# Two halves of the tokens, taken differently: five matmuls per weight tile in place of six in a float32 decoder step

## The chip, the cores and the metric

One core of a Trainium2 chip runs the whole program. Its engines are TensorE (PE in the profile; its weight loads have a row of their own, PEld), VectorE (DVE), ScalarE (ACT), GpSimd (POOL) and SyncE (SP, which issues most DMAs). Each engine works through its own queue in the order of issue, and semaphores tie the queues together. The metric is the time of one execution on the device, in microseconds; lower is better.

## The reference

One step of a two-layer decoder trunk over 520 tokens: a prompt of 512 and eight samples of one token each. Everything is float32. Cut to what matters:

```python
def layer(x, ...):
    x = x + 0.5 * swiglu_ffn(rms_norm(x, p['ffn1_norm']), wg, wu, wd)     # 1024 -> 2816 -> 1024
    h = rms_norm(x, p['mix_norm'])
    z = h @ p['w_in']              # 1024 -> 2560, split into
    # retention q, k, v, gate | windowed attention q, k, v | a gated pair for a convolution
    ...
    y = jnp.concatenate([o_r, o_a, o_c], axis=-1) @ p['w_out']           # 1024 -> 1024
    x = x + y
    x = x + 0.5 * swiglu_ffn(rms_norm(x, p['ffn2_norm']), wg2, wu2, wd2)
```

The outputs are the 520 tokens' vectors and the new states of retention, attention window and convolution.

## The kernel before

**Layout.** Activations lie with features on the 128 partitions and tokens along the columns: `x` is `[128, 8, 520]`. Weights come in tiles of 128 x 128, eight to a chunk of 512 KB, in the order of their use; a chunk is one DMA.

**Three terms for a product.** The big products are done on float32r operands, rounded forms of float32. To keep float32's accuracy each operand is split into two float32r parts, high and low: for weights by a ScalarE copy (line 185, `wh`) and a VectorE subtraction (line 192, `wl`), for the inputs likewise (`xh`, `xl`; lines 252 and 254, 222 and 223 for the FFN's hidden values `hs`). The product is `wh*xl + wh*xh + wl*xh`. `mm3` (line 206) issues this for one weight tile. An output tile `o` takes two banks of PSUM of 512 float32 columns each, and the 520 tokens are halved: 260 columns go to the first bank, 260 to the second (`HN` = 260). So a weight tile costs three terms times two halves, six matmuls, each with its own weight load:

```python
def mm3(o, w, vh, vl, first, last):
    for i, (a, b) in enumerate(((w[0], vl), (w[0], vh), (w[1], vh))):
        for s in range(2):
            nc.tensor.matmul(o[:, s, :HN], lhsT=a, rhs=b[:, s * HN : (s + 1) * HN], ...)
```

**Stages.** Each layer is an FFN, the mix and a second FFN. In an FFN (`ffn`, line 277) two groups of 11 blocks `f` are made: eight tiles of the gate into `og`, eight of the up projection into `ou`, then `silu(og * R) * (ou * R)` with the norm's factors `R` (lines 288 to 294), split into two parts. Then for each of eight output blocks `m` eleven tiles are summed and added to `x` (line 299). After the second group the next stage's input is prepared block by block (`prep`, line 250), and the next stage starts while the last blocks are being prepared.

The mix has 20 blocks of the input projection (`in_tile`, eight tiles each; RQ, RK, RV, RG of retention, AQ, AK, AV of attention, CA and CG of the convolution), the three mechanisms themselves, and the output projection in two halves of four tiles for each of eight blocks (`out`; steps `a` and `b`). Blocks that are scaled by `R` go through one VectorE operation that reads both banks (lines 380, 388, 484, 765, 851); others are copied by one ScalarE operation (lines 514, 663, 682); the convolution's pointwise product is split straight from PSUM (lines 461 and 464); the output projection is added to `x` at line 881. The order of all these steps on all queues is written out by hand in `ORDER` (line 80), where `t` is a part of the convolution's 62 taps on VectorE, `h` and `l` are the two halves of splitting the next chunk of weights, `s` and `n` are steps of the prompt's attention and of retention's norms.

**Buffers.** PSUM holds four output tiles `o` of two banks, which is all of it. Three chunks of raw weights and three of split ones are held. 20 units of 1040 columns hold intermediates.

Of the kernel before, what the change touches and what calls it, by code (L numbers as in the profile page):

```python
# [19 lines left out]
HN = NT // 2  # L20
FFN = 2816
# [9 lines left out]
# Columns of the packed per-layer parameters.  # L31
# [8 lines left out]
# Columns of the packed constants that depend on shapes alone.  # L40
# [37 lines left out]
# The mix's steps in the order of their issue. A step comes in parts, and each mention of it issues  # L78
# its next part. h and l stand for the two halves of the split of the next chunk of weights.
# [35 lines left out]
def step_kernel(ctx: ExitStack, tc: tile.TileContext, io: dict):  # L115
# [15 lines left out]
    xh = const.tile([128, KD, NT], F32R, name="xh")  # L131
    xl = const.tile([128, KD, NT], F32R, name="xl")
# [33 lines left out]
    # ---- the stream of 128x128 weight tiles in the order of their use: chunks are loaded, then  # L166
    # split exactly into two float32r parts ----
# [9 lines left out]
    def split_hi(i):  # L177
        """The first part of chunk i; the second is left pending."""
        if i == nxt[0] and i < NCH:
            nxt[0] += 1  # L180
            ensure_load(i)
            t, raw[i] = raw[i], None
            h = wspl.tile([128, CT * 128], F32R, tag="wh", name="wh")
            lo = wspl.tile([128, CT * 128], F32R, tag="wl", name="wl")
            nc.scalar.copy(h, t)  # L185
            spl[i] = (h, lo)
            pending.append((i, t))
# [18 lines left out]
    def mm3(o, w, vh, vl, first, last):  # L206
        for i, (a, b) in enumerate(((w[0], vl), (w[0], vh), (w[1], vh))):
            for s in range(2):
                nc.tensor.matmul(  # L209
                    o[:, s, :HN], lhsT=a, rhs=b[:, s * HN : (s + 1) * HN],  # L210
                    start=first and i == 0, stop=last and i == 2,
                )
# [37 lines left out]
    def prep(l, gain, k):  # L250
        g = prm(l, gain, k)
        nc.scalar.activation(xh[:, k], x[:, k], AF.Copy, scale=g)  # L252
        yield
        nc.vector.scalar_tensor_tensor(  # L254
            xl[:, k], x[:, k], g, xh[:, k].bitcast(F32), op0=ALU.mult, op1=ALU.subtract
        )
# [20 lines left out]
    def ffn(norm, after):  # L277
        for g in range(NG):
            hs = []
            for f in range(GF):  # L280
                first = g == 0 and f == 0
                og, ou = ptile(), ptile()
                for o, k in ffn_tiles(first, og, ou):
                    mm3(o, next_tile(), xh[:, k], xl[:, k], k == 0, k == KD - 1)
# [10 lines left out]
            for m in range(KD):  # L295
                o = ptile()
                for f in range(GF):
                    mm3(o, next_tile(), hs[f][:, 0], hs[f][:, 1], f == 0, f == GF - 1)
# [6 lines left out]
    def mix(l, after):  # L305
# [19 lines left out]
        def in_tile():  # L325
            o = ptile()
            for k in range(KD):
                mm3(o, next_tile(False), xh[:, k], xl[:, k], k == 0, k == KD - 1)
# [6 lines left out]
        # Each step is a generator, whose parts each keep to one engine for the most.  # L335
# [8 lines left out]
        def decayed():  # L344
            """The norm's factors times the decay of retention's queries."""
# [8 lines left out]
        def token_scales():  # L354
            """The norm's factors, and those with the decay of keys, with tokens on the partitions."""
# [13 lines left out]
        def conv_a(c):  # L369
# [10 lines left out]
            nc.vector.scalar_tensor_tensor(v2(a), o[:, :, :HN], 0.5, v2(R), op0=ALU.mult, op1=ALU.mult)  # L380
# [3 lines left out]
        def conv_g(c):  # L384
# [3 lines left out]
            nc.vector.tensor_mul(v2(g), o[:, :, :HN], v2(R))  # L388
# [32 lines left out]
        def conv_rest():  # L421
# [18 lines left out]
            hi, lo = two(unit(F32R)), two(unit(F32R))  # L440
            table(SILU)
            for c in range(2):
# [3 lines left out]
                nc.scalar.copy(hi[:, c], y[:, c])  # L446
            yield
            for c in range(2):
                nc.vector.tensor_sub(lo[:, c], y[:, c], hi[:, c].bitcast(F32))
            yield  # L450
            os = []
            for m in range(2):
                o = ptile()
                os.append(o)
                for k in range(2):
                    s = slice(k * 256 + m * 128, k * 256 + m * 128 + 128)
                    mm3(o, (pw[0][:, s], pw[1][:, s]), hi[:, k], lo[:, k], k == 0, k == 1)
            yield
            hl = two(unit(F32R)), two(unit(F32R))
# [19 lines left out]
        def att_qk(g):  # L479
            """Queries of a group or, where g is None, keys, with an RMS norm over each half of the partitions."""  # L480
# [3 lines left out]
            nc.vector.tensor_mul(v2(a), o[:, :, :HN], v2(R))  # L484
# [25 lines left out]
        def att_v():  # L510
# [3 lines left out]
            nc.scalar.copy(v2(av), o[:, :, :HN])  # L514
# [18 lines left out]
        def att_out():  # L533
            return get(att, "o", lambda: (two(unit(F32R)), two(unit(F32R))))
# [7 lines left out]
        def att_prompt(n):  # L542
            """128 queries: scores, softmax with the sink, values."""
# [54 lines left out]
            h_, l_ = (t[:, :, n * 128 : (n + 1) * 128] for t in att_out())  # L598
            src = o[:, 0, :256].rearrange("p (g t) -> p g t", g=2)
            nc.scalar.copy(h_, src)  # L600
            yield
            nc.vector.tensor_sub(l_, src, h_.bitcast(F32))
# [10 lines left out]
        def att_sample():  # L613
# [34 lines left out]
            for v in range(2):  # L648
                s = slice(64 * v, 64 * v + 64)
                src = o[s, 0, :32].rearrange("p (b v g) -> p v g b", b=NB, v=2)[:, v]  # L650
                part.append([src] + [t[s, :, SEQ:] for t in att_out()])
                nc.scalar.copy(part[v][1], src)
# [6 lines left out]
        def ret_k(a):  # L659
# [3 lines left out]
            nc.scalar.copy(v2(kT), o[:, :, :HN])  # L663
# [14 lines left out]
        def ret_v(h):  # L678
# [3 lines left out]
            nc.scalar.copy(v2(vT), o[:, :, :HN])  # L682
# [38 lines left out]
        def ret_state(a):  # L721
            """The samples' new states: a step of the recurrence."""
# [11 lines left out]
        def ret_kv():  # L734
            """The prompt's states after each 128 tokens."""
# [25 lines left out]
        def ret_q(a):  # L761
# [3 lines left out]
            nc.vector.tensor_mul(v2(q), o[:, :, :HN], v2(Rd[:, a]))  # L765
# [8 lines left out]
        def ret_prompt(c0):  # L774
            """The outputs of 256 tokens."""
# [71 lines left out]
        def ret_gate(h):  # L847
# [3 lines left out]
            nc.vector.tensor_mul(v2(sg), o[:, :, :HN], v2(R))  # L851
# [5 lines left out]
        def ret_out(h):  # L857
            """The gated outputs, whose two parts take the place of those of the input."""
# [3 lines left out]
            hi, lo = ret["hl", h] = xh[:, h], xl[:, h]  # L862
            nc.scalar.copy(hi, sg)
            yield
            nc.vector.tensor_sub(lo, sg, hi.bitcast(F32))
            yield

# [1 line left out]
        def row_input(name):  # L869
# [3 lines left out]
            h_, l_ = (att if name[0] == "A" else conv)["o"]  # L873
            return h_[:, j], l_[:, j]

        def out(names, m, last):
            o = ptile()
            for i, n in enumerate(names):
                mm3(o, next_tile(False), *row_input(n), i == 0, i == len(names) - 1)
            yield  # L880
            nc.vector.tensor_add(v2(x[:, m]), v2(x[:, m]), o[:, :, :HN])
# [112 lines left out]
def host_arrays(i):  # L994
    """The inputs in the kernel's layouts."""
# [6 lines left out]
    def cols(w):  # L1002
        """(L, K, M) -> (L, M/128, 128 of K, K/128, 128 of M)"""
# [92 lines left out]
```

## Time and profile before

| | |
|---|---|
| median of 3 runs | 2007.87 us (2006.96 to 2008.45) |
| span of the profiled execution, first to last instruction | 2003.0 us |
| busy share of TensorE, VectorE, ScalarE, GpSimd | 98%, 49%, 33%, 1% |
| matmuls recorded | 16,190, of them 15,360 on line 209 |
| mean granted clock of TensorE | 0.991 |
| DMA | 188 MB, mean 94 GB/s |

The profile gives no time of the profiled execution apart from its span; the time shown is that of the runs, so 4.9 us lie outside the span. Two stretches of 200 us differ from the rest: 400 to 600 and 1400 to 1600 us are the two mixes; what is left is the four FFNs. A row of a group reads: line, engine, operation, output tile <- input tiles, shapes, count | busy us, mean ns of one | idle time just before them and who ended it.

### The profile page before, as it was taken

The page shows a single profiled execution, that of the slowest core. Times are in us where ns is not written, and L with a number is a line of the kernel's source. Part 1 is how long each engine was busy: PE and PEld are TensorE (multiplying, and loading weights), DVE is VectorE, ACT ScalarE, POOL GpSimd, SP SyncE. Part 2 cuts the span into 40 slices and gives each one's busy share as a digit, 9 for nine tenths or more (in the row PEclk, how much of TensorE's full clock was granted, in tenths as well). Part 3 has the DMA queues.
Part 4 walks back from the last instruction along what each step waited for, and adds up shares of the span by engine and source line. Part 5 has one row for each costly group of instructions (what it writes and reads, how often), then busy time and mean ns, then how long its engine had stood idle before and what let it go on. Part 6 is the DMA issues. An engine that isn't in the chain of part 4 may idle for free. (4 is left out here: it accounts for less than half of the span.)

```text
span 2003.0 us, 36435 instructions
## 1 busy us (share of the span) xinstructions
PE 1963.1 (98%) x16190; PEld 1942.6 (97%) x16190; DVE 983.8 (49%) x1311; ACT 665.6 (33%) x960; POOL 27.1 (1%) x52
## 2 busy tenths in 40 slices
PE   8999999989989999999999999999899899999999
PEld 8999999989979999999999999999898899999999
DVE  6442444568666443344444434445786564434442
ACT  5221223423664221222332212234236642212221
POOL 0000000000100000000000000000001000000000
PEclk9999999999999999999999999999899999999999
DMA  5222222233402222222222222222333122222221
GB/s 189 100 85 95 85 95 95 94 99 103 128 31 87 96 95 95 85 96 95 90 90 86 99 90 96 85 95 86 118 101 108 43 95 85 96 95 87 93 101 70
DMA packets 64415, 188.21 MB, mean 94 GB/s; under 512 B 12450, under 2 KB 18818, under 8 KB 64130
## 3 DMA queue, kind: packets, MB, share of 16 engines
q1 hardware_dynamic: 61554, 178.37, 26.0%
q0 software_dynamic: 2560, 7.41, 1.5%
q8 instruction: 127, 2.08, 0.4%
q14 instruction: 30, 0.25, 0.0%
q10 hardware_dynamic: 144, 0.11, 0.0%
HBM read 178.42 MB, written 7.43 MB: 93 GB/s over the span
## 5 line engine op out<-in xcount | busy, mean ns | idle before, releaser
L209 PE MATMUL o<-xl,wh 128*128 128x260 f32 x3584 | 727.7, 284 | 14.4 <-ACT wh L185 7.2
L209 PE MATMUL o<-xh,wl 128*128 128x260 f32 x3584 | 725.9, 284 | 1.9 <-DVE wl L192 1.9
L209 PE MATMUL o<-xh,wh 128*128 128x260 f32 x3584 | 724.9, 284 | 0.0
L192 DVE TENSOR_TENSOR wl<-w,wh 128x1024 fp32r<-128x1024 f32 x318 | 388.9, 1224 | 450.9 <-ACT wh L185 448.9
L209 PEld LDWEIGHTS o<-xl,wh 128*128 128x128 f32 x3584 | 556.9, 190 | 16.0 <-ACT wh L185 7.6
L209 PEld LDWEIGHTS o<-xh,wl 128*128 128x128 f32 x3584 | 556.2, 190 | 2.8 <-DVE wl L192 2.8
L209 PEld LDWEIGHTS o<-xh,wh 128*128 128x128 f32 x3584 | 555.3, 190 | 0.0
L185 ACT CAST wh<-w 128x1024 fp32r<-128x1024 f32 x318 | 333.2, 1049 | 616.0 <-PE o L209 298.9
L209 PE MATMUL o<-m,wh 128*128 128x260 f32 x3072 | 493.0, 282 | 0.0
L209 PEld LDWEIGHTS o<-m,wh 128*128 128x128 f32 x3072 | 421.0, 188 | 0.0
L209 PE MATMUL o<-m,wl 128*128 128x260 f32 x1536 | 308.7, 282 | 0.0
L209 PEld LDWEIGHTS o<-m,wl 128*128 128x128 f32 x1536 | 236.5, 188 | 0.0
L291 DVE TENSOR_TENSOR u<-o,R 128x520 f32<-128x520 f32 x88 | 61.5, 699 | 248.3 <-PE o L209 248.3
L222 ACT CAST m<-u 128x520 fp32r<-128x520 f32 x88 | 55.2, 627 | 324.3 <-DVE u L292 324.3
L290 ACT ACTIVATE t<-t 128x520 f32<-128x520 f32 x88 | 56.2, 638 | 164.3 <-DVE t L288 164.3
L299 DVE SCALAR_TENSOR_TENSOR x<-o,x 128x520 f32<-128x520 f32 x64 | 44.7, 698 | 97.9 <-PE o L209 97.6
L223 DVE TENSOR_TENSOR m<-u,m 128x520 fp32r<-128x520 f32 x88 | 61.6, 700 | 61.1 <-ACT m L222 61.1
L410 DVE SCALAR_TENSOR_TENSOR m<-m,par 128x512 f32<-128x512 f32 x120 | 90.0, 750 | 2.9
L252 ACT ACTIVATE xh<-x,par 128x520 fp32r<-128x520 f32 x48 | 34.9, 729 | 99.1 <-DVE x L299 80.2
L292 DVE TENSOR_TENSOR u<-u,t 128x520 f32<-128x520 f32 x88 | 61.7, 701 | 9.2
L288 DVE TENSOR_TENSOR t<-o,R 128x520 f32<-128x520 f32 x88 | 60.9, 692 | 0.1
L254 DVE SCALAR_TENSOR_TENSOR xl<-x,par,xh 128x520 fp32r<-128x520 f32 x48 | 36.3, 757 | 21.3 <-ACT xh L252 21.3
(166 smaller groups left out, 668.2 us busy)
## 6 DMA issues: line engine op xcount, KB each, us to landing
w<-in_w SPq DMA_DIRECT2D x318, 512.0 KB, 3.2
out_y<-x SPq DMA_DIRECT2D x8, 260.0 KB, 2.4
m<-in_s_ret SPq DMA_DIRECT2D x8, 256.0 KB, 6.1
m<-sc POOLq DMA_DIRECT2D x8, 256.0 KB, 4.4
out_o_rets<-m POOLq DMA_DIRECT2D x8, 256.0 KB, 4.1
x<-in_x SPq DMA_DIRECT2D x3, 520.0 KB, 6.4
cc<-in_cc SPq DMA_DIRECT2D x1, 1092.0 KB
w<-in_w SPq DMA_DIRECT2D x4, 256.0 KB, 5.6
```

Of the source, the lines that this page charges most:

```text
L185: nc.scalar.copy(h, t)
L192: nc.vector.tensor_sub(lo, t, h.bitcast(F32))
L209: nc.tensor.matmul(o[:, s, :HN], lhsT=a, rhs=b[:, s * HN : (s + 1) * HN], start=first and i == 0, stop=last and i == 2,)
L222: nc.scalar.copy(h, src)
L223: nc.vector.tensor_sub(lo, src, h.bitcast(F32))
L254: nc.vector.scalar_tensor_tensor(xl[:, k], x[:, k], g, xh[:, k].bitcast(F32), op0=ALU.mult, op1=ALU.subtract)
L288: nc.vector.tensor_mul(v2(t), og[:, :, :HN], v2(R))
L290: nc.scalar.activation(t, t, AF.Silu)
L291: nc.vector.tensor_mul(v2(u), ou[:, :, :HN], v2(R))
L292: nc.vector.tensor_mul(u, u, t)
L299: nc.vector.scalar_tensor_tensor(v2(x[:, m]), o[:, :, :HN], 0.5, v2(x[:, m]), op0=ALU.mult, op1=ALU.add)
L410: nc.vector.scalar_tensor_tensor(y[:, :SEQ], ub[:, j : j + SEQ], w, y[:, :SEQ], op0=ALU.mult, op1=ALU.add)
```

## The change

`NT` = 520 tokens are no longer halved but cut at `NA` = 280; the other part has `NBK` = 240. The inputs' two parts lie in one tile, high beside low (`xs[128, 8, 2, 520]` in place of `xh` and `xl`; `hs[f]` and the mix's inputs alike). For a weight tile:

- the 280 tokens take the three terms one by one, three matmuls of 280 columns into the first bank;
- the 240 tokens take `wh*xh` and `wh*xl` in one matmul of 2 x 240 = 480 columns into the second bank, side by side, and `wl*xh` in one of 240 columns, which is accumulated onto the low side.

An output tile thus comes in three pieces: 280 finished columns in the first bank, and in the second 240 + 240 that are still to be added. Three helpers empty a tile: `scaled` (ScalarE copies one piece, VectorE multiplies the 280, adds the other piece and multiplies the 240), `copied` (two ScalarE copies and a VectorE addition) and `added` (three VectorE operations onto `x`). The convolution's pointwise output is first made whole and then split; the attention's two parts, now in one tile for each head group, are written by two operations instead of one. The order of steps, the loads and the weights' layout stay. Comments are dropped too.

```diff
+NA = 280
+NBK = NT - NA
...
-    xh = const.tile([128, KD, NT], F32R, name="xh")
-    xl = const.tile([128, KD, NT], F32R, name="xl")
+    xs = const.tile([128, KD, 2, NT], F32R, name="xs")
...
-    def mm3(o, w, vh, vl, first, last):
-        for i, (a, b) in enumerate(((w[0], vl), (w[0], vh), (w[1], vh))):
-            for s in range(2):
-                nc.tensor.matmul(
-                    o[:, s, :HN], lhsT=a, rhs=b[:, s * HN : (s + 1) * HN],
-                    start=first and i == 0, stop=last and i == 2,
-                )
+    def mm3(o, w, v, first, last):
+        pa, pb, pl = o[:, 0, :NA], o[:, 1, : 2 * NBK].rearrange("p (a t) -> p a t", a=2), o[:, 1, NBK : 2 * NBK]
+        nc.tensor.matmul(pa, lhsT=w[0], rhs=v[:, 1, :NA], start=first, stop=False)
+        nc.tensor.matmul(pa, lhsT=w[0], rhs=v[:, 0, :NA], start=False, stop=False)
+        nc.tensor.matmul(pb, lhsT=w[0], rhs=v[:, :, NA:], start=first, stop=False)
+        nc.tensor.matmul(pa, lhsT=w[1], rhs=v[:, 0, :NA], start=False, stop=last)
+        nc.tensor.matmul(pl, lhsT=w[1], rhs=v[:, 0, NA:], start=False, stop=last)
+
+    def halves(o):
+        return o[:, 0, :NA], o[:, 1, :NBK], o[:, 1, NBK : 2 * NBK]
+
+    def scaled(dst, o, r, c=None):
+        pa, ph, pl = halves(o)
+        nc.scalar.copy(dst[:, NA:], pl)
+        if c is None:
+            nc.vector.tensor_mul(dst[:, :NA], pa, r[:, :NA])
...
+        nc.vector.tensor_add(dst[:, NA:], dst[:, NA:], ph)
+        if c is None:
+            nc.vector.tensor_mul(dst[:, NA:], dst[:, NA:], r[:, NA:])
...
+    def copied(dst, o):
+        pa, ph, pl = halves(o)
+        nc.scalar.copy(dst[:, NA:], pl)
+        nc.scalar.copy(dst[:, :NA], pa)
+        nc.vector.tensor_add(dst[:, NA:], dst[:, NA:], ph)
+
+    def added(dst, o, c):
+        pa, ph, pl = halves(o)
+        for d, p in ((dst[:, :NA], pa), (dst[:, NA:], pl), (dst[:, NA:], ph)):
+            nc.vector.scalar_tensor_tensor(d, p, c, d, op0=ALU.mult, op1=ALU.add)
...
-                nc.vector.tensor_mul(v2(t), og[:, :, :HN], v2(R))
+                scaled(t, og, R)
...
-                nc.vector.tensor_mul(v2(u), ou[:, :, :HN], v2(R))
+                scaled(u, ou, R)
...
-                nc.vector.scalar_tensor_tensor(
-                    v2(x[:, m]), o[:, :, :HN], 0.5, v2(x[:, m]), op0=ALU.mult, op1=ALU.add
-                )
+                added(x[:, m], o, 0.5)
...
             for m, o in enumerate(os):
-                nc.scalar.copy(v2(hl[0][:, m]), o[:, :, :HN])
-            yield
-            for m, o in enumerate(os):
-                nc.vector.tensor_sub(v2(hl[1][:, m]), o[:, :, :HN], v2(hl[0][:, m]).bitcast(F32))
+                copied(y[:, m], o)
+            yield
+            for m in range(2):
+                nc.scalar.copy(hi[m], y[:, m])
+            for m in range(2):
+                nc.vector.tensor_sub(lo[m], y[:, m], hi[m].bitcast(F32))
...
-            nc.scalar.copy(h_, src)
-            yield
-            nc.vector.tensor_sub(l_, src, h_.bitcast(F32))
+            for g in range(2):
+                nc.scalar.copy(out[g][:, 0], o[:, 0, g * 128 : (g + 1) * 128])
+            yield
+            for g in range(2):
+                nc.vector.tensor_sub(out[g][:, 1], o[:, 0, g * 128 : (g + 1) * 128], out[g][:, 0].bitcast(F32))
...
-            nc.vector.tensor_add(v2(x[:, m]), v2(x[:, m]), o[:, :, :HN])
+            added(x[:, m], o, 1.0)
```

In the mix `scaled` takes the place of the operations on lines 380, 388, 484, 765 and 851, and `copied` of those on lines 514, 663 and 682.

More of the change, by code (lines that the diff above doesn't have):

```diff
@@ L283, in ffn @@
                 for o, k in ffn_tiles(first, og, ou):
-                    mm3(o, next_tile(), xh[:, k], xl[:, k], k == 0, k == KD - 1)
+                    mm3(o, next_tile(), xs[:, k], k == 0, k == KD - 1)
                 if first:
@@ L297, in ffn @@
                 for f in range(GF):
[L298 to L301 removed]
+                    mm3(o, next_tile(), hs[f], f == 0, f == GF - 1)
+                added(x[:, m], o, 0.5)
                 if g == NG - 1:
@@ L327, in in_tile @@
             for k in range(KD):
-                mm3(o, next_tile(False), xh[:, k], xl[:, k], k == 0, k == KD - 1)
+                mm3(o, next_tile(False), xs[:, k], k == 0, k == KD - 1)
             return o
@@ L379, in conv_a @@
             a = wt("ca")
-            nc.vector.scalar_tensor_tensor(v2(a), o[:, :, :HN], 0.5, v2(R), op0=ALU.mult, op1=ALU.mult)
+            scaled(a, o, R, 0.5)
             conv[c] = a, ub, us
@@ L387, in conv_g @@
             g = wt("cg")
-            nc.vector.tensor_mul(v2(g), o[:, :, :HN], v2(R))
+            scaled(g, o, R)
             yield
@@ L439, in conv_rest @@
             yield
-            hi, lo = two(unit(F32R)), two(unit(F32R))
+            hl = [two(unit(F32R)) for _ in range(2)]
+            hi, lo = ([t[:, i] for t in hl] for i in range(2))
             table(SILU)
@@ L445, in conv_rest @@
                 )
-                nc.scalar.copy(hi[:, c], y[:, c])
+                nc.scalar.copy(hi[c], y[:, c])
             yield
             for c in range(2):
-                nc.vector.tensor_sub(lo[:, c], y[:, c], hi[:, c].bitcast(F32))
+                nc.vector.tensor_sub(lo[c], y[:, c], hi[c].bitcast(F32))
             yield
@@ L483, in att_qk @@
             a = wt("az")
-            nc.vector.tensor_mul(v2(a), o[:, :, :HN], v2(R))
+            scaled(a, o, R)
             yield
@@ L513, in att_v @@
             av = unit()[:, :NT]
-            nc.scalar.copy(v2(av), o[:, :, :HN])
+            copied(av, o)
             yield
@@ L533, in att_out @@
         def att_out():
-            return get(att, "o", lambda: (two(unit(F32R)), two(unit(F32R))))
+            return get(att, "o", lambda: [two(unit(F32R)) for _ in range(2)])
         def neg_max(out, scores, bias, nsink, ng):
@@ L597, in att_prompt @@
             yield
-            h_, l_ = (t[:, :, n * 128 : (n + 1) * 128] for t in att_out())
-            src = o[:, 0, :256].rearrange("p (g t) -> p g t", g=2)
-            nc.scalar.copy(h_, src)
+            out = [t[:, :, n * 128 : (n + 1) * 128] for t in att_out()]
+            for g in range(2):
+                nc.scalar.copy(out[g][:, 0], o[:, 0, g * 128 : (g + 1) * 128])
             yield
-            nc.vector.tensor_sub(l_, src, h_.bitcast(F32))
+            for g in range(2):
+                nc.vector.tensor_sub(out[g][:, 1], o[:, 0, g * 128 : (g + 1) * 128], out[g][:, 0].bitcast(F32))
             yield
@@ L649, in att_sample @@
                 s = slice(64 * v, 64 * v + 64)
-                src = o[s, 0, :32].rearrange("p (b v g) -> p v g b", b=NB, v=2)[:, v]
-                part.append([src] + [t[s, :, SEQ:] for t in att_out()])
-                nc.scalar.copy(part[v][1], src)
+                for g in range(2):
+                    src = o[s, 0, :32].rearrange("p (b v g) -> p v g b", b=NB, v=2)[:, v, g]
+                    part.append((src, att_out()[g][s, 0, SEQ:], att_out()[g][s, 1, SEQ:]))
+                    nc.scalar.copy(part[-1][1], src)
             yield
@@ L662, in ret_k @@
             kT = get(ret, "kT", lambda: two(unit()))[:, a]
-            nc.scalar.copy(v2(kT), o[:, :, :HN])
+            copied(kT, o)
             yield
@@ L681, in ret_v @@
             vT = wt("vT")
-            nc.scalar.copy(v2(vT), o[:, :, :HN])
+            copied(vT, o)
             yield
@@ L764, in ret_q @@
             q = get(ret, "q", lambda: two(unit()))[:, a]
-            nc.vector.tensor_mul(v2(q), o[:, :, :HN], v2(Rd[:, a]))
+            scaled(q, o, Rd[:, a])
             yield
@@ L850, in ret_gate @@
             sg = get(ret, ("g", h // 2), lambda: two(unit()))[:, h % 2]
-            nc.vector.tensor_mul(v2(sg), o[:, :, :HN], v2(R))
+            scaled(sg, o, R)
             yield
@@ L861, in ret_out @@
             yield
-            hi, lo = ret["hl", h] = xh[:, h], xl[:, h]
-            nc.scalar.copy(hi, sg)
+            hl = ret["hl", h] = xs[:, h]
+            nc.scalar.copy(hl[:, 0], sg)
             yield
-            nc.vector.tensor_sub(lo, sg, hi.bitcast(F32))
+            nc.vector.tensor_sub(hl[:, 1], sg, hl[:, 0].bitcast(F32))
             yield
@@ L878, in out @@
             for i, n in enumerate(names):
-                mm3(o, next_tile(False), *row_input(n), i == 0, i == len(names) - 1)
+                mm3(o, next_tile(False), row_input(n), i == 0, i == len(names) - 1)
             yield
-            nc.vector.tensor_add(v2(x[:, m]), v2(x[:, m]), o[:, :, :HN])
+            added(x[:, m], o, 1.0)
             yield
```

14 lines of the change are left out of this document (8 added, 6 removed).

## The prediction

> **What bounds the kernel now.** I read the page first (busy shares, then the costliest groups), then stretches of the span with the granted clock, then the waits of TensorE, and last the order of time in three places.
>
> ```profile
> span 2003.0 us, 36435 instructions
> ...
> PE 1963.1 (98%) x16190; PEld 1942.6 (97%) x16190; DVE 983.8 (49%) x1311; ACT 665.6 (33%) x960; POOL 27.1 (1%) x52
> ...
> L209 PE MATMUL o<-xl,wh 128*128 128x260 f32 x3584 | 727.7, 284 | 14.4 <-ACT wh L185 7.2
> L209 PE MATMUL o<-xh,wl 128*128 128x260 f32 x3584 | 725.9, 284 | 1.9 <-DVE wl L192 1.9
> L209 PE MATMUL o<-xh,wh 128*128 128x260 f32 x3584 | 724.9, 284 | 0.0
> ...
> L209 PE MATMUL o<-m,wh 128*128 128x260 f32 x3072 | 493.0, 282 | 0.0
> ...
> L209 PE MATMUL o<-m,wl 128*128 128x260 f32 x1536 | 308.7, 282 | 0.0
> ```
>
> TensorE is busy for 98% of the span, and nearly all of that is line 209, the six matmuls of a weight tile: 3 x 3584 + 3072 + 1536 = 15,360, so 2560 tiles. The groups hardly ever sit idle. The 282 to 284 ns are one matmul's record from start to modelled end and overlap, so the pace has to come from a full stretch:
>
> ```profile
> 200.00:400.00 200.00, 200.00 (x1670) 200.00 (x1669) 90.55 (x107) 63.52 (x80) 0.00 (x0) 1.00 0.27 92
> 400.00:600.00 200.00, 184.11 (x1475) 174.30 (x1475) 139.19 (x242) 94.24 (x189) 13.07 (x22) 0.97 0.31 89
> ```
>
> (Columns: stretch, length, then busy us and count of PE, weight loads, DVE, ACT and POOL, then the granted clock.) In an FFN stretch TensorE never rests and takes 200/1670 = 119.8 ns a matmul, six to a tile, 719 ns. VectorE is at 45% and ScalarE at 32% there. In the mix (400 to 600) TensorE loses 16 us and VectorE rises to 70%. So FFN time is matmul pace alone; the mix is shared.
>
> **The change part by part.** *Columns.* Before, a tile streams 6 x 260 = 1560 columns. After, 3 x 280 + 480 + 240 = 1560. Not one column is saved; what goes is one instruction and its weight load. So the question is how much of 119.8 ns belongs to the instruction and how much to its columns. The trace shows the same matmul at half clock, after a stall:
>
> ```profile
> 425.27 0.64 PE L209 MATMUL o<-xl,wh 128*128 128x260 f32 x2
> ...
> 427.00 0.64 PE L209 MATMUL o<-xh,wh 128*128 128x260 f32 x2
> ```
>
> ```profile
> 424.60:426.00 1.40, 1.38 (x7) 1.33 (x7) 1.36 (x3) 1.13 (x2) 0.13 (x1) 0.50 0.27 73
> ```
>
> Between these two rows lie four pairs (the rows at 425.27, 425.70, 426.13 and 426.57): 1.73 us for eight matmuls, 216 ns each at clock 0.50. That is 0.83 ns a column, so 0.416 at full clock, and 260 columns should take 108.2 ns. They take 119.8: 11.6 ns too much, which half clock does not show. The bounds are therefore 0 saved per tile (the excess goes with the columns, a limit of the stream at full speed) and 11.6 saved (it goes with the instruction, through its start or the load beside it). No matmul of this type with another width is in the trace. A plain cost per instruction should have shown at half clock too, which speaks against the upper end; a load of about 113 ns (below) beside a stream of 108 but only a part of one of 480 speaks against the lower one. Neither row is nearer, so I take 7 ns, a little above the middle, and keep both ends.
>
> The Trainium skill, TensorE: Matmul & The Clock Gate, section Back-to-back issue gap, gives a warm gap of N/2.4 + 2.5 ns. By it a tile would save one 2.5, an estimate of 5.5 us over 2220 tiles, and the time would be 2012 with the mix below; that lies in the stretch of rival A and shares its chance. This trace has 119.8 where that rule has 110.8, so it lacks most of the excess in question.
>
> *Where the saving counts.* From the code, an FFN has 11 x 2 x 16 + 2 x 8 x 11 = 528 tiles; four have 2112, the mixes 2 x 224. In the mixes I count only a quarter of the tiles, 110, since VectorE paces a third of a mix and fixed waits eat some of the rest. 2220 x 7 ns = 15.5 us gained (ends 0 and 25.8).
>
> *Adding the halves.* The rows for it:
>
> ```profile
> L881 DVE TENSOR_TENSOR x<-x,o 128x520 f32<-128x520 f32 x32 | 22.0, 692 | 25.8 <-PE o L209 25.6
> L602 DVE TENSOR_TENSOR m<-o,m 128x256 fp32r<-128x256 f32 x8 | 3.3, 415 | 5.8 <-ACT m L600 5.8
> L682 ACT COPY vT<-o 128x520 f32<-128x520 f32 x8 | 4.7, 582 | 0.0
> L600 ACT CAST m<-o 128x256 fp32r<-128x256 f32 x8 | 2.9, 368 | 7.4 <-PE o L592 7.4
> ```
>
> From 692 and 415 ns a VectorE column costs 1.05 ns: 240 columns 0.40 us, 280 0.44. From 582 and 368, ScalarE's 240 cost 0.355 and 280 0.39. So `scaled` goes from one operation of 0.69 to 0.44 + 0.40 + 0.40 = 1.24 on VectorE (+0.54) and adds 0.355 on ScalarE; `added` goes likewise to 1.24 (+0.54); `copied` goes from 0.58 to 0.745 on ScalarE (+0.16) and adds 0.40 on VectorE.
>
> In an FFN a column block f lasts 16 x 0.72 = 11.5 us and gets two `scaled`: 1.1 us more on VectorE, 0.7 on ScalarE, beside a VectorE that is 55% idle. The new ScalarE copy waits for the group's last matmul; behind it in ScalarE's queue stand the next weight splits, which are made more than one chunk of 5.75 us ahead. The last h is used ten tiles (7.2 us) after its chain of now about 4 us begins. Four output buffers turn over every 5.75 us or slower. Cost nothing; without the cover it would be 88 x 1.1 = 97 us, which would take a VectorE at 100%. `added` after the last down tile lengthens by 0.54 the way to the next input, which has 7 tiles of cover, save at the end of the program: +0.5. No DMA and no queue is moved.
>
> *The mix.*
>
> ```profile
> 424.00:492.00 68.00, 63.90 (x505) 63.04 (x504) 64.00 (x93) 18.45 (x29) 2.46 (x4) 0.95 0.32 102
> ```
>
> ```profile
> PE o L580 <- ACT m L574: 9.3, 2, 4.6
> PE o L333 <- DVE rt L362: 8.0, 2, 4.1
> PE o L209 <- ACT wh L185: 7.2, 2, 4.8
> ```
>
> From 424 to 492 us VectorE works 64.0 of 68 us (the convolution's taps between weight splits). Into this stretch fall seven `scaled` (CA1, CG1, RQ0, RQ1, RG0, AQ0, AQ1) and five `copied` (RV0 to RV3, RK1): 7 x 0.54 + 5 x 0.40 = 5.8 us more on the engine that has 4 us to spare. TensorE already waits there for an output buffer that VectorE empties at line 362, 4.1 us a layer. Ahead of that point stand two `scaled` and four `copied`: 2.7 us more, all of it waited for. Of the other 3.1 I take half. With 0.5 for the prompt attention, whose two parts are now written by two operations instead of one (0.16 on ScalarE and 0.15 on VectorE more, four times a layer), a layer costs 4.7: 9.4 for two. Ends: 2 if later waits of other cause shrink by as much, 18 if the eight later `added` that meet the softmax are paid too. The convolution's own output is ready some 2 us later and is used 50 us on: nothing.
>
> *Sum.* The profiled span is 2003.0; the median of the runs is 2007.87, so 4.9 us lie around the span and stay. 2007.9 - 15.5 + 0.5 + 9.4 = 2002.3.
>
> **The rivals.**
>
> *A, slower: the excess goes with the columns.* The place is every matmul of 280 or 480 columns: 0.461 ns a column throughout, and nothing is saved, or little (under 3.5 ns a tile). Then only VectorE's share in the mix is left: 2007.9 + 9.9 = 2017.8. It decides from under about 2.6 ns saved a tile (2220 x 2.6 = 5.8, leaving +4). For it speaks the half-clock row; against it, that one load fewer must be worth something if loads and streams get in each other's way.
>
> *B, slower: the weight load bounds the short stream.*
>
> ```profile
> 514.68 1.88 PEld L824 LDWEIGHTS o<-su,m 128*128 128x128 f32 x16
> ```
>
> Sixteen loads with almost no columns to stream: (1.88 - 0.19)/15 = 113 ns each, the last one's record being 0.19. A stream of 240 columns is 100 ns at 0.416, shorter than the load of the next weight. If the 240 then take the 119.8 of today while the rest goes by columns (0.461), a tile gains 119.8 - 110.6 = +9.2 ns: 2220 x 9.2 = 20 us, so 2038. The Trainium skill, TensorE: Matmul & The Clock Gate, section LDWEIGHTS, has P/1.2 ns for P columns, an estimate of 106.7 for 128. The row has 113, and both put a stream of 240 columns below the load: this rule speaks against the change.
>
> *C, much faster: the loads are the bound already.* If 119.8 is the load's pace and not the stream's, the three matmuls of 280 columns and the one of 240 take 119.8 each and the 480 columns their 200: 679 against 719, 40 x 2220 = 89 us, so 2017.8 - 89 = 1929. Against it: the load alone took 113, not 120.
>
> *D, much slower: under 260 columns the fast form is lost.* Every matmul of this type here has 260 columns; plain float32 is slower:
>
> ```profile
> 550.68 1.14 PE L228 MATMUL o<-rsq,one 128*128 128x260 f32 x4 [0.83 <-ACT rsq L837]
> ```
>
> These four records are two float32 matmuls of 260 columns (line 228 issues two a sum), 1.14/2 = 0.57 us each at most. If one of 240 went that way, 0.53 us in place of 0.11, a tile would lose 0.42 us: 2560 x 0.42 = 1075 us, so about 3090. Nothing in the trace speaks for it but that no narrower one is there.
>
> **How the numbers follow.** A measurement of this kernel can tell about 0.2%, 4 us, from no change: below 2003.9 is faster, above 2011.9 slower. My forecast, a part of the excess saved, has 0.60. Its own range is 1987 (11.6 saved a tile, 25.8, mix and end +5) to 2018 (3.5 saved, 8, mix +18): faster 0.42, same 0.13, slower 0.05. Rival A 0.24: same 0.10, slower 0.14. B 0.06, slower. C 0.05, faster. D 0.05, slower. Together faster 0.47, same 0.23, slower 0.30. The range takes in the forecast's own, A (2017.8, to 2026 with the mix at its upper end) and leaves out B, C and D: 1987 to 2026.
>
> **What would show it.** After: 2560 x 5 = 12,800 matmuls in mm3; in a full FFN stretch a tile of five in 712 ns (719 = A, 679 = C, 728 = B, over 1000 = D), so 142.4 ns a matmul; VectorE at some 55% there and no new idle time of TensorE; in the mix a wait of TensorE for line 362's successor of 6 to 7 us a layer. If FFN tiles come out near 708, the upper end was right and the time is near 1993. Wrong altogether would be an FFN stretch in which TensorE waits for VectorE or ScalarE, or a mix that loses more than 18 us.

## The result, and the profile after

The changed kernel takes 2034.2 us (median of 4 runs, 2026.5 to 2035.9) against 2007.4 for the kernel before (2006.7 to 2008.5): a ratio of 1.0126, 95% interval 1.0109 to 1.0144. It is slower by 1.3%, where 0.3% faster was forecast, and lies 8 us outside the range.

The page after, first the span and the engines' busy time, then the five matmuls' groups on the scaled input:

```profile
span 2032.0 us, 32138 instructions
...
PE 1982.2 (98%) x13622; PEld 1876.6 (92%) x13622; DVE 1128.7 (56%) x1937; ACT 728.9 (36%) x1196; POOL 27.1 (1%) x52
...
L214 PE MATMUL o<-xs,wh 128*128 128x480 f32 x1792 | 684.6, 382 | 0.0
...
L212 PE MATMUL o<-xs,wh 128*128 128x280 f32 x1792 | 533.0, 297 | 17.2 <-ACT wh L186 9.4
L215 PE MATMUL o<-xs,wl 128*128 128x280 f32 x1792 | 526.2, 294 | 3.9 <-DVE wl L193 3.8
L213 PE MATMUL o<-xs,wh 128*128 128x280 f32 x1792 | 526.1, 294 | 0.0
...
L216 PE MATMUL o<-xs,wl 128*128 128x240 f32 x1792 | 494.7, 276 | 0.0
```

2568 matmuls fewer are issued, one for each tile (the prediction's 2560 left out the convolution's eight pointwise tiles; line 209 had 15,408 matmuls, not 15,360), and TensorE is busy for 19 us more. That can't come from columns, which are equal in number. The three stretches that the prediction used:

```profile
200.00:400.00 200.00, 200.00 (x1396) 191.79 (x1396) 105.40 (x169) 70.94 (x102) 0.00 (x0) 1.00 0.30 92
400.00:600.00 200.00, 179.61 (x1158) 160.82 (x1156) 143.67 (x275) 94.50 (x206) 13.09 (x22) 0.89 0.30 85
424.00:492.00 68.00, 62.42 (x422) 59.20 (x421) 65.19 (x105) 18.86 (x39) 2.46 (x4) 0.93 0.31 92
```

In the FFN TensorE still takes all of 200 us; 200/1396 = 143.3 ns a matmul is 716.3 ns a tile, against 718.6 before. VectorE is at 53%, ScalarE at 35%, and TensorE waits for nobody. In the mix the granted clock fell from 0.97 to 0.89. The mean clock of the whole execution, after and then before:

```profile
core 0: 2032.0 us, clock 0.978
```

```profile
core 0: 2003.0 us, clock 0.991
```

Since the clock here is either 1 or 0.5, this is 2 x 0.022 x 2032 = 89 us at half clock, against 2 x 0.009 x 2003 = 36. Cut at the first matmul of each stage (and the last FFN at its last tile), the four FFNs went from 1524.5 to 1519.6 us (-4.9), and the two mixes from 233.3 and 234.6 to 250.6 each (+33.3).

The waits of TensorE after (us in total, times, longest):

```profile
PE o L364 <- DVE su L720: 10.5, 2, 5.6
...
PE o L614 <- ACT m L608: 7.8, 2, 4.4
...
PE o L215 <- DVE wl L193: 3.8, 2, 1.9
PE o L843 <- DVE m L787: 2.3, 2, 1.2
PE o L736 <- DVE az L229: 1.5, 2, 0.8
```

The wait that the prediction named (line 362's successor) grew by 1.3 us a layer, VectorE's weight splits are waited for 3.8 us in place of 1.9, and the last two waits are new. All of this is some 4 us a layer, far from 16.6. What else happened in layer 0 stands in the order of time, TensorE first:

```profile
545.81 0.38 PE L838 MATMUL o<-m 128*128 128x128 f32 x2
547.34 0.48 PE L843 MATMUL o<-m 64*128 64x128 f32 x2 [1.16 <-DVE m L787]
...
549.01 0.49 PE L843 MATMUL o<-m 64*128 64x128 f32 x2
549.42 0.74 PE L838 MATMUL o<-m 128*128 128x128 f32 x2
550.10 0.79 PE L843 MATMUL o<-m 64*128 64x128 f32 x2
```

and VectorE:

```profile
544.40 0.94 DVE L239 TENSOR_TENSOR m<-m,o 128x240 f32<-128x240 f32 x2 [1.78 <-ACT m L238]
545.72 1.31 DVE L497 TENSOR_TENSOR m<-m 128x520 fp32r<-128x520 f32 x2 [0.39 <-ACT m L495]
546.95 1.63 DVE L787 SCALAR_TENSOR_TENSOR m<-m,cc,o 128x128 f32<-128x128 f32 x6
```

The small matmuls of retention's outputs wait 1.16 us for the retention state (line 787), because the sum and the split of the convolution's output (lines 239 and 497) stand ahead of it on VectorE. The split now waits for ScalarE's copies and for the sum: in layer 0 it ends 3.6 us after the last pointwise matmul, where it had ended 1.4 us after it. Two microseconds later a pair of these matmuls takes 0.79 us where it had taken 0.49. The stretch that follows, and the one before the change that begins with the same work:

```profile
549.50:570.00 20.50, 20.50 (x66) 14.61 (x67) 5.02 (x18) 6.45 (x14) 1.87 (x4) 0.50 0.20 66
```

```profile
538.00:558.50 20.50, 17.54 (x99) 12.72 (x97) 10.98 (x33) 13.13 (x29) 3.42 (x6) 1.00 0.27 86
```

After, the clock is at 0.50 for 20.5 us, TensorE is busy throughout and issues 66 matmuls; before, it was at 1.00, issued 99 and was idle for 3 us. Layer 1 has the same from 1559.9 to 1576.9 us.

### The profile page after: what moved, and what is told of

It is laid out like the page before. It is cut to its first block, busy times and chain, and to the rows that moved or that the text cites. A ratio compares the mean times of both kernels' runs of the same rounds, so it can differ in the third digit from the quotient of the medians.

```text
span 2032.0 us, 32138 instructions
## 1 busy us (share of the span) xinstructions
PE 1982.2 (98%) x13622; PEld 1876.6 (92%) x13622; DVE 1128.7 (56%) x1937; ACT 728.9 (36%) x1196; POOL 27.1 (1%) x52
## 3 DMA queue, kind: packets, MB, share of 16 engines
q0 software_dynamic: 2560, 7.41, 1.5%
## 4 chain that ended last, share of the span: by engine, by line
PE 86%; DVE 7%; DMA 4%; ACT 2%; issue 2%; SPq 0%; POOL 0%; DVEq 0%; ACTq 0%; POOLq 0%
PE o L214 25%; PE o L212 15%; PE o L215 15%; PE o L213 15%; PE o L216 13%; DVE m L441 3%; DMA w<-in_w 3%; DVE wl L193 1%; PE o L838 1%; PE o L261 1%; PE o L843 1%; DMA m<-sc 0%; ACT wh L186 0%; DVE nt L279 0%; PE o L860 0%
## 5 line engine op out<-in xcount | busy, mean ns | idle before, releaser
L214 PE MATMUL o<-xs,wh 128*128 128x480 f32 x1792 | 684.6, 382 | 0.0
L212 PE MATMUL o<-xs,wh 128*128 128x280 f32 x1792 | 533.0, 297 | 17.2 <-ACT wh L186 9.4
L215 PE MATMUL o<-xs,wl 128*128 128x280 f32 x1792 | 526.2, 294 | 3.9 <-DVE wl L193 3.8
L213 PE MATMUL o<-xs,wh 128*128 128x280 f32 x1792 | 526.1, 294 | 0.0
L216 PE MATMUL o<-xs,wl 128*128 128x240 f32 x1792 | 494.7, 276 | 0.0
L216 PEld LDWEIGHTS o<-xs,wl 128*128 128x128 f32 x1792 | 338.7, 189 | 53.0
L212 PEld LDWEIGHTS o<-xs,wh 128*128 128x128 f32 x1792 | 340.7, 190 | 19.1 <-ACT wh L186 9.8
L215 PEld LDWEIGHTS o<-xs,wl 128*128 128x128 f32 x1792 | 340.9, 190 | 5.6 <-DVE wl L193 5.5
L213 PEld LDWEIGHTS o<-xs,wh 128*128 128x128 f32 x1792 | 343.1, 191 | 0.2
L214 PEld LDWEIGHTS o<-xs,wh 128*128 128x128 f32 x1792 | 341.7, 191 | 0.0
L214 PE MATMUL o<-m,wh 128*128 128x480 f32 x768 | 292.1, 380 | 0.0
L212 PE MATMUL o<-m,wh 128*128 128x280 f32 x768 | 225.1, 293 | 0.0
L213 PE MATMUL o<-m,wh 128*128 128x280 f32 x768 | 223.5, 291 | 0.0
L215 PE MATMUL o<-m,wl 128*128 128x280 f32 x768 | 223.4, 291 | 0.0
L216 PE MATMUL o<-m,wl 128*128 128x240 f32 x768 | 209.5, 273 | 0.0
```

The costliest lines, as they stand in the source:

```text
L212: nc.tensor.matmul(pa, lhsT=w[0], rhs=v[:, 1, :NA], start=first, stop=False)
L213: nc.tensor.matmul(pa, lhsT=w[0], rhs=v[:, 0, :NA], start=False, stop=False)
L214: nc.tensor.matmul(pb, lhsT=w[0], rhs=v[:, :, NA:], start=first, stop=False)
L215: nc.tensor.matmul(pa, lhsT=w[1], rhs=v[:, 0, :NA], start=False, stop=last)
L216: nc.tensor.matmul(pl, lhsT=w[1], rhs=v[:, 0, NA:], start=False, stop=last)
```

## The experiments

My first theory from this: the FFN gives 2.3 ns a tile; the rest is the mix, where added evacuation work delays VectorE, and short waits in a stretch of little TensorE work let the clock fall. Rivals: the FFNs lose something too; the matmul form itself costs in the mix; the falling clock is a neighbour of the wait and not its effect.

### Which part: FFN or mix

Edits are given in short here and below.

```diff
 e1: kernel before, and in the FFNs alone
-    xh, xl: two arrays [128, KD, NT]
+    xs = const.tile([128, KD, 2, NT], F32R, name="xs"); xh, xl = xs[:, :, 0], xs[:, :, 1]
-    mm3(...) and its one-operation evacuation
+    five matmuls, scaled(), added()
 e2: changed kernel, and in the FFNs alone the old mm3 and evacuation
```

> Five matmuls per tile in the four FFNs alone; the mix keeps its six matmuls of 260 columns and its evacuation in one operation. Theory (the matmul pace gives about 2.3 ns a tile, 2112 tiles = 4.9 us, and the whole loss lies in the mix): the median falls to about 2002.5, 0.2 to 0.3% below before; mix layers at 233 to 235 us as before; the granted clock is at half for about 38 us, as before. Rival (the longer evacuation costs TensorE time in the FFNs too, or the five matmuls lower the clock there): 2007 or more, with new half-clock stretches or waits inside the FFNs.

Measured: 2000.3 us, ratio 0.9967 (0.9954 to 0.9979); FFNs 1518.9 us in all, mixes 236.3 and 231.7. As expected, a little better.

> The reverse: the FFNs keep six matmuls of 260, the mix has all of the change. Theory: 2034.2 + 4.9 = 2039, mix layers at about 250 us and half clock for about 90 us, as in the changed kernel. Rival (the two parts act on each other, for example through weight chunks split later by the FFN): clearly below 2030, mix layers under 245 us.

Measured: 2025.7 us (runs at 2022.4, 2022.8, 2028.6 and 2028.7), 1.0098 (1.0083 to 1.0114). A miss of 13 us, for two reasons. In the profiled run only layer 1 had the long half-clock stretch (mixes 243.5 and 251.2), though TensorE waited for the state in both, 2.3 us in all; the two runs at 2028.6 and 2028.7 have a lower mean clock, 0.976 against 0.982. And its FFNs, with the old six matmuls of 260, took 1515.1 us: 9.4 us less than the kernel before and 4.5 less than with five matmuls. In what TensorE reads there, nothing differs from the kernel before but the place of the scaled input in SBUF. That opened a second question, taken up below.

### Is it the evacuation, and is it the late state

```diff
 e3: changed kernel, in the mix alone
-    scaled(), copied(), added() in three or four operations
+    one operation over o[:, :, :HN], the two parts not summed
 e4: changed kernel, the written order
-    RK0 kv cv kv cv kv AK0
+    RK0 kv cv kv kv cv AK0
 e13: e3 and e4 together
```

> The changed kernel with all its five-matmul tiles, but in the mix each output buffer is emptied in one operation of 520 columns, as before, and the two parts of the last 240 tokens are not summed (the mix's values are wrong for that reason; its work in matmuls is unchanged). Theory (the added VectorE and ScalarE work of the evacuation is what delays TensorE and lets its clock fall): most of the 33 us of the mix comes back, median 2003 to 2010, mix layers 233 to 238, half clock for 35 to 55 us. Rival (the form of the matmuls in the mix, or the regrouped split of the attention and convolution outputs, is what costs): 2022 or more, mix layers at 245 or more.

Measured: median 2011.2, just outside the theory's range, but on three levels: three runs at 2002.4 to 2002.8, four at 2009.3 to 2011.9, three at 2017.5 to 2019.7. Their mean clocks are 0.989 to 0.990, 0.984 to 0.987 and 0.980 to 0.981. The profiled run, from the middle level, had mixes of 243.3 and 235.3, and in layer 0 alone a half-clock stretch of 17 us; the state was waited for in both layers (1.7 us in all). So without the added evacuation a layer is as short as before, unless the clock falls, which costs 8 us a layer and here comes in some executions only. The other two levels have no trace; that they are no fall and two falls is read from their clocks.

> The changed kernel with one change in the written order: the retention state's copy and VectorE step go ahead of the split of the convolution output's parts (two steps change places), so that TensorE should no longer wait 1.16 us for the state (line 787). Theory (that short wait, in a stretch of small matmuls, is what drops the clock for 20.5 and 17.1 us): the long half-clock stretch goes or shrinks to 7 us or less in both layers, each mix layer is 7 to 10 us shorter, median 2014 to 2020. Rival (the clock would fall there anyway, the wait is its neighbour only): 1.2 us a layer come back, median 2031 to 2033.

Measured: 2016.6 us, ratio 1.0051 (1.0037 to 1.0064): 17.6 us back for two steps that change places. The state no longer appears among the waits, mixes are 242.9 and 241.7, and the stretch runs at full clock:

```profile
540.00:560.00 20.00, 18.94 (x131) 14.67 (x131) 10.61 (x28) 12.77 (x28) 4.54 (x8) 1.00 0.33 101
```

> The changed kernel with the retention state's step ahead of the convolution's split (as in the run of that name), and in the mix each output buffer emptied in one operation without the sum of the two parts (the mix's values are wrong for that). Theory (what is left of the mix's loss without the late state, 9.6 and 7.1 us a layer against before, is the added evacuation): mix layers at 233 to 237 us, median 2001 to 2004, all runs on one level, with no half-clock stretch of 17 us or more. Rival (the five-matmul form or the regrouped splits cost something in the mix by themselves): mix layers at 239 to 243, median 2010 to 2017.

Measured: 2002.8 us, ratio 0.9981 (0.9971 to 0.9991), eight of ten runs from 2001.7 to 2003.2, mixes 235.2 and 234.7. So the matmul form costs 2.0 us at most in the mix. The 33.3 us are 16.7 for the late state (250.6 x 2 less 242.9 + 241.7), 14.7 for the evacuation (to 235.2 + 234.7), and 2.0 left. What the 14.7 consist of is seen in the waits of the kernel with the state first:

```profile
PE o L364 <- DVE su L720: 11.0, 2, 5.6
...
PE o L215 <- DVE wl L193: 4.3, 3, 1.9
...
PE o L736 <- DVE az L229: 1.5, 2, 0.8
```

and of the one without the sums:

```profile
PE o L376 <- DVE rt L405: 8.8, 2, 4.6
...
PE o L215 <- DVE wl L193: 0.9, 2, 0.7
```

2.2 + 3.4 + 1.5 = 7.1 us are these waits. The mean clocks, 0.986 and 0.990, make 2 x 0.004 x 2015 = 16 us more at half clock, worth up to 8. That share is worked out; no run shows it alone.

### Does a short wait bring the clock down

Two runs turn the cause around: a wait added to the kernel before, and work added to the changed one.

```diff
 e5: kernel before, ret_kv
-            for c in range(1, 4):
+            for c in (1, 1, 1, 1, 2, 3):
 e10: changed kernel, ret_prompt, ahead of the outputs' matmuls
+            if c0 == 2:
+                for i in range(5):
+                    nc.tensor.matmul(o[:, i % 2], lhsT=pw[0][:, :128], rhs=xs[:, 7, 0, :512], start=True, stop=True)
```

> The kernel before with one small addition: the first two VectorE operations of the retention state's step (line 751) are issued four times instead of once (the same result each time), 6 x 0.27 = 1.6 us more on VectorE, so that TensorE waits there by some 1.2 to 1.6 us, as it does in the changed kernel; nothing else is touched. Theory (a wait of a microsecond inside this stretch of small matmuls brings a half-clock stretch of about 20 us, worth some 8 us): one or both layers show a half-clock stretch of 17 us or more, the median at 2015 (one layer) or 2024 (both), single runs on levels some 8 us apart. Rival (the wait costs its own length): 2009 to 2010, half-clock time about 38 us as before.

Measured: 2014.1 us (2013.5, 2013.6, 2014.6, 2020.1), ratio 1.0041 (1.0025 to 1.0056), near the theory's figure for one layer. The wait came out at 0.7 us a layer, about half of what was expected; layer 1 of the profiled run:

```profile
1535.65 0.38 PE L802 MATMUL o<-m 128*128 128x128 f32 x2
1536.73 0.48 PE L807 MATMUL o<-m 64*128 64x128 f32 x2 [0.69 <-DVE m L751]
...
1538.39 0.49 PE L807 MATMUL o<-m 64*128 64x128 f32 x2
1538.81 0.80 PE L802 MATMUL o<-m 128*128 128x128 f32 x2
1539.54 0.79 PE L807 MATMUL o<-m 64*128 64x128 f32 x2
```

The same picture as in the changed kernel: 2.1 us after the end of the wait the pairs go from 0.49 to 0.80 us. The clock stays down for 20.5 us, and this mix takes 241.8 us instead of 234.6. Layer 0 had the same wait and kept its clock: 235.2 us instead of 233.3. The same wait of 0.7 us thus went with 1.9 us in one layer and 7.2 in the other.

> The changed kernel, order of steps untouched, with five matmuls of 512 columns put ahead of the retention outputs (their results are overwritten by the matmuls that follow): about 1.1 us of TensorE work at the place where it waits 1.16 us for the retention state. Theory (the granted clock falls because too little is computed in that stretch): the clock stays up there, the long half-clock stretches of 20.5 and 17.1 us go, the median falls to 2015 to 2020 although the state comes as late as before. Rival (it falls for the lateness or the order of the steps themselves): 2034, stretches as before.

Measured: 2021.5 us (2019.8 to 2022.4), ratio 1.0073 (1.0056 to 1.009): 12.7 us faster than the changed kernel, with more work, though 1.5 us above the expected range. The state comes as late: its operation on VectorE starts 1.15 us after the filler does, as it had started 1.14 us after the outputs' first matmul. In the place of the wait:

```profile
547.10 1.33 PE L834 MATMUL o<-xs,pwh 128*128 128x512 f32 x5
548.26 0.38 PE L841 MATMUL o<-m 128*128 128x128 f32 x2
548.64 0.48 PE L846 MATMUL o<-m 64*128 64x128 f32 x2
```

```profile
547.00:567.00 20.00, 18.75 (x104) 13.63 (x102) 11.87 (x34) 12.73 (x28) 3.42 (x6) 1.00 0.29 90
```

The clock is at 1.00 from 547 to 567 us, neither layer has a half-clock stretch over 6.8 us, and all four runs have the same mean clock, 0.986. It is 4.9 us short of the reordered kernel: mixes 244.5 and 244.9, since the five matmuls take their 1.2 us themselves; the rest stays open. With this the clock's fall is shown to follow from what TensorE does there, not from the lateness or the order.

What exactly counts is not shown: the five matmuls both fill the gap and add work. The gap alone it is not. In the changed kernel the clock also fell at 1532.55 us, after 3.4 us (1529.14 to 1532.55) in which TensorE's records leave no gap; 28 of the 32 matmuls there have two columns (line 860). And it stayed down through 20.5 us in which TensorE was never idle.

### What a removed matmul is worth

A gate and up stretch, 825 to 935 us, at full clock in all kernels. Before:

```profile
825.00:935.00 110.00, 110.00 (x918) 110.00 (x918) 49.42 (x58) 32.01 (x39) 0.00 (x0) 1.00 0.26 90
```

```diff
 e7: kernel before, layout alone
-    xh, xl: two arrays [128, KD, NT]
+    xs = const.tile([128, KD, 2, NT], F32R, name="xs"); xh, xl = xs[:, :, 0], xs[:, :, 1]
 e8: e7 with rows padded: xs = [128, KD, 2, 576], :NT used
 e6b: e1 with six matmuls: 280, 280, 280 into one bank, 240, 240, 240 into the other
 e9: e1 with xs = [128, 2, KD, NT], the old layout
 e11: e1 with NA = 264
 e12: e6b with NA = 264
```

> The kernel before with all its six matmuls of 260 and its evacuation; only the two parts of the scaled input lie in one array, a part beside the other for each 128 rows, as in the changed kernel. Theory (the place of the moving operand in SBUF sets part of a matmul's 119.8 ns; in the kernel with six matmuls in the FFNs and this layout a gate or up tile took 713.3 ns against 720.9): 1408 gate and up tiles x 7.6 = 10.7 us less and something in the mix, median 1993 to 1997. Rival (that pace came from something else of that kernel, such as its other buffers): 2004 to 2008, gate and up tiles at 719 to 721.

Measured: 1997.9 us, ratio 0.9951 (0.9938 to 0.9963), with nothing but the place of an array changed. It is 0.9 us above the theory's range; the gate and up tiles took 713.4 ns, and the mix, at 235.4 and 233.9, gained nothing.

```profile
825.00:935.00 110.00, 110.00 (x927) 110.00 (x927) 50.20 (x58) 32.20 (x40) 0.00 (x0) 1.00 0.28 92
```

927 matmuls in place of 918 (records overlap, so each count holds some two from the edges).

> As the layout run, but each row of 520 columns is padded to 576 (2304 bytes, nine times 256), so that all rows start at the same place of a 256-byte line. If the pace depends on the start address within 256 bytes, the eight row blocks k, which in the run with 2080-byte rows differ by 710.6, 715.9, 711.7 and 716.4 ns a tile with a period of four, all take the same time here, somewhere from 700 to 725. If the differences come from VectorE's and ScalarE's work, which repeats with the eight tiles of a weight chunk, they stay, with a period of eight. The total is 1985 to 2010 by which of the places is hit.

Measured: 2006.6 us, 0.9995 (0.9986 to 1.0004). All eight row blocks take 720.0 ns a tile, to the tenth, where the layout run had 710 to 716 with a period of four. So in these layouts a tile's time follows where its rows start within 256 bytes; a rhythm of VectorE and ScalarE, which would have stayed, is not the cause.

> The kernel with the change in the FFNs alone, where each tile has six matmuls again, three of 280 and three of 240 columns (the 480 columns as two matmuls of 240, which lets all three terms of the last 240 tokens add up in the buffer, so the evacuation is two operations and no sum). Same layout and the same columns as with five, one instruction and one weight load more. If an instruction has a price of its own (5.4 ns, from 111.8 ns for 240 columns and 218.2 for 480), a gate or up tile takes about 724 ns against 718.3 and the time is 2011. If the number of instructions is worth nothing (columns and the place of the operands set the pace), tiles stay within 3 ns of 718 and the time within 5 us of 2000.

Measured: 2019.5 us, 1.007 (1.0055 to 1.0085): 19 us more than with five, and beyond both readings; a gate or up tile took 729.9 ns.

```profile
825.00:935.00 110.00, 110.00 (x907) 110.00 (x907) 48.38 (x73) 30.54 (x37) 0.00 (x0) 1.00 0.26 92
```

Of the difference only 3.8 ns lie at the two matmuls that became one: from start to next start 111.7 + 110.0 ns for 240 columns twice, 217.9 for 480. The rest is that the neighbours, with unchanged columns, take less (131.8 and 132.7 became 129.2 and 128.8, 112.8 became 111.7).

> Five matmuls per tile in the FFNs alone, as in the run that did this before, but the two parts of the scaled input lie as in the kernel before: all first parts, then all second parts. With it there are four kernels: six or five matmuls, old or new layout; gate and up tiles took 720.9 ns (six, old), 713.3 (six, new) and 718.3 (five, new). If five matmuls cost nothing or gain nothing and the place of the operands decides, the tile falls somewhere in 710 to 725 and differs from 718.3. If the form alone set 718.3, it is 718.3 again and the time 2000.

Measured: 2000.4 us, 0.9971 (0.9959 to 0.9982). The tile is 718.3 ns again; single row blocks differ from the run with the new layout (715 to 721 against 713 to 723), the mean does not.

> Five matmuls per tile in the FFNs alone, split at 264 and 256 tokens in place of 280 and 240 (the long stream has 512 columns). So far, for a gate or up tile in this layout: six of 260 columns 713.3 ns, six of 280 and 240 columns 729.9, five 718.3: the removed instruction is worth 11.6 ns and the uneven split costs 16.6. Theory (a split near the even one costs little, and the instruction's 11.6 ns is then kept): 702 to 708 ns a tile, 2112 tiles x 10 to 16 ns under e1's, median 1967 to 1985. Rival (the split's 16.6 is a matter of where the second part of the row begins, and this one begins at another unlucky or lucky place): 712 to 725, median 1990 to 2012.

Measured: 1995.7 us, ratio 0.9949 (0.9935 to 0.9962): the rival's range, not the theory's.

> Six matmuls per tile in the FFNs, three of 264 and three of 256 columns, same layout. If the cost of the uneven split grows with its unevenness (a short stream waits for the next weight load of 113 ns while a long one gains nothing from it), it is 4/20 of 16.6 or less: a gate or up tile at 713 to 717 ns. If the removed instruction is worth 11.6 ns here too, the five-matmul run of this split is 11.6 ns below this one. If the place decides, it is anywhere from 710 to 735.

Measured: 2001.5 us, 0.9974 (0.9964 to 0.9984); a gate or up tile took 718.3 ns, above the first reading's 713 to 717, and the removed matmul is worth 3.3 ns here, not 11.6.

Together, in ns a tile from the starts of successive tiles, over the four FFNs, from one profiled run each (down tiles read another array, whose layout is the same in all):

| matmuls of a tile | input's layout | gate and up | down | run |
|---|---|---|---|---|
| 6: 260 each | old | 720.8 | 718.6 | before |
| 6: 260 each | new | 713.4 | 718.6 | e7 |
| 6: 260 each | padded | 720.0 | 718.5 | e8 |
| 6: 280 and 240 | new | 729.9 | 724.3 | e6b |
| 5: 280, 480, 240 | new | 718.3 | 716.2 | e1 |
| 5: 280, 480, 240 | old | 718.3 | 716.2 | e9 |
| 6: 264 and 256 | new | 718.3 | 720.5 | e12 |
| 5: 264, 512, 256 | new | 715.0 | 717.8 | e11 |

All eight stream 1560 columns. The removed matmul is worth 11.6 and 8.1 ns at 280 and 240, but 3.3 and 2.7 at 264 and 256. The uneven split costs 16.5 and 5.7 ns, or 4.9 and 1.9. The new layout is worth 7.4 with six matmuls of 260 and nothing with five. What the operand's place and the pieces' lengths do to each other inside the chip is not settled by these runs; that they matter as much as the number of instructions is.

The Trainium skill, TensorE: Matmul & The Clock Gate, section Wait — 56ns, not 53.3ns?, has one fixed cost of some 2.5 ns a matmul at full clock. The 3.3 and 2.7 ns are near it, the 11.6 and 8.1 are not, and 7.4 ns by layout alone is nothing that a price per matmul can give.

The two fastest versions can't be told apart: the kernel before with the new layout (e7), and five matmuls at 264 tokens in the FFNs alone (e11), both 0.5% faster than before. The first is a change of two lines. Five matmuls at 280 tokens in the FFNs alone (e1) are 0.3% faster.

## Why the prediction was wrong

*Columns and the price of a matmul (first step).* The failing step is "Not one column is saved; what goes is one instruction and its weight load", as if nothing else changed. Pieces of 280 and 240, in the new layout, cost 9.1 ns a tile more than pieces of 260 in the kernel before (729.9 against 720.8): 16.5 for the pieces, less 7.4 for the layout. From these, five matmuls in place of six take back 11.6. That this equals the upper end of the prediction is luck: there it was the excess of a single matmul over its columns, and the same removal is worth 8.1 on down tiles and 3.3 at 264 tokens. The term of 7 ns measured 2.3 (4.9 us over 2112 tiles), the 15.5 us were 4.9.

*Rivals.* A was nearest on the FFN: 719 was its figure, 716.3 came. Its reason was not what the runs showed: the excess belongs neither to the column nor to the instruction alone (0.465 ns a column at 240, 0.454 at 480). B, C and D fell: the streams of 240 on gate and up tiles start 111.7 ns before the next matmul, not 119.8; tiles are far from 679; and no form was lost.

*Evacuation in the FFN.* Right: no wait, VectorE 53% against 55% forecast, and the durations as worked out (0.44, 0.40, 0.40 and 0.355 us):

```profile
L226 DVE TENSOR_TENSOR u<-o,R 128x280 f32<-128x280 f32 x88 | 39.6, 450 | 238.7 <-ACT u L224 238.7
...
L231 DVE TENSOR_TENSOR u<-u,R 128x240 f32<-128x240 f32 x88 | 36.0, 409 | 3.0
...
L229 DVE TENSOR_TENSOR u<-u,o 128x240 f32<-128x240 f32 x88 | 34.7, 395 | 0.0
L224 ACT COPY u<-o 128x240 f32<-128x240 f32 x88 | 31.5, 358 | 145.9 <-PE o L216 145.9
```

The 0.5 us at the end of the program came too: from the last matmul's end to the end of the span, 4.0 us became 4.5.

*The mix.* This step decided: 9.4 us were forecast and 33.3 came. For the added evacuation alone it was 14.7. The mechanism of added waits held, and they sum to 7.1: the wait at line 362 grew by 1.3 a layer and not by 2.7, while the weight splits took more. The rest, up to 8, is clock, for which the step had no term; that 14.7 lies inside its ends, 2 and 18, is in that part luck. What the step did not have at all is the late state, 16.7 us. "The convolution's own output is ready some 2 us later and is used 50 us on: nothing" was true of that output and wrong in what it left out: its sum and split, which now end later, stand in VectorE's queue ahead of the retention state, which TensorE uses at once. And each wait was priced at its own length, although the profile before had shown matmuls at clock 0.50 after a stall; that row I used for a price per column only.

In the profiled spans 2003.0 - 4.9 + 14.7 + 16.7 + 2.0 + 0.5 gives 2032.0, as measured. The prediction's 4.9 us around the span were a misreading: the runs last 1.8 us longer than their spans (2033.8 against 2032.0), and the profiled execution before was a quick one. Three runs of the changed kernel took 2033.8 to 2035.9; the fourth, 2026.5, lies 8 us below, about the price of one half-clock stretch, and its mean clock is 0.981 against their 0.978.

## What to carry to other kernels

Ask of every wait that a change adds not only how long it is but what TensorE's activity is around it: beside small matmuls, waits of 0.7 to 1.2 us cost 7 to 8 us wherever the clock fell with them, and either another order of two steps or filler matmuls took most of it back. When an evacuation gets longer, look at what stands behind it in its engine's queue, not only at who reads its result. And when a change also moves an operand, run the move by itself: here it was worth more in the FFN than the five matmuls.

## What the hardware showed that I had not expected

- The clock fell some 2 us after waits of 1.16 and 0.69 us. The Trainium skill, TensorE: Matmul & The Clock Gate, section HAM oscillation — how this bites in real kernels, warns of idle gaps over some 3.4 us. Here gaps of a third and a fifth of that were enough, in a stretch of matmuls of 128 columns that alone kept the clock. Lengths agree with that page's window of 3.41 us (section What's actually happening): the half-clock stretches measured 3.41, 6.83, 17.07, 20.48 and 23.89 us, 1, 2, 5, 6 and 7 of them.
- Much the same wait can go either way: in the mix without the sums (e3) the clock fell in one layer and not in the other, after a wait of 0.8 us in each, and the runs lie on levels 8 us apart. What decides between the two is not shown.
- Six matmuls of 260 columns at full clock took from 710 to 741 ns a tile from one row block of the input to the next in the kernel before (709.9 to 740.9), and 720.0 in all eight once their rows started at the same place within 256 bytes.
